# An encoder layer on one core: first-pass weights fetched a pair ahead, weight sums in three steps, a buffer pool moved, output row tiles alternated

## The chip, the core and the metric

The kernel runs on one core of one Trainium2 chip, in float32. The metric is the device time of one execution in microseconds (us). The engines each work through a queue of their own in order: PE (TensorE) multiplies matrices, DVE (VectorE) and ACT (ScalarE) work elementwise, SP (SyncE) issues nearly all DMAs.

## The reference

```python
mod = jax.nn.silu(c) @ w_ada + b_ada
shift, scale, gate = jnp.split(mod, 3, axis=-1)
h = rmsnorm(x, pre_g) * (1.0 + scale[:, None]) + shift[:, None]
q, k, v, gate_a, u, gate_p = jnp.split(h @ w_in, SPLIT_POINTS, axis=-1)
y_a = windowed_gqa(q, k, v, rel_table, sink) * jax.nn.silu(gate_a)
y_p = multiscale_pool(u, w_pool_grp, pool_scale) * jax.nn.silu(gate_p)
g_a, g_p = jnp.split(jax.nn.sigmoid(h @ w_merge + b_merge), 2, axis=-1)
merged = g_a * (y_a @ w_br_attn) + g_p * (y_p @ w_br_pool)
return x + gate[:, None] * rmsnorm(merged @ w_out, post_g)
```

There are 1024 rows of x, the model width is 2048, the combined projection is 4608 columns wide and the merge projection 4096; y_a and y_p are 1024 wide. Everything is float32. The attention sees 128 keys on either side; the pool takes windows of 2 to 16 rows.

## The kernel before, in words

A float32 product is made of three products in a rounded format (float32r). Each operand is split into a high part, written by ACT (L91), and a low part, the rest, written by DVE (L92); PE adds high by high, low by high and high by low. Both parts of a weight are called `whi` and `wlo`, those of the moving operand by the name of the operand and an h or l (`T4h`, `T4l`).

On top of that, a block product of 2 by 2 blocks is made of seven products instead of eight (Strassen's scheme in Winograd's form, `strassen`). The moving operands of the seven are, in order, B11, T3, T2, B21, T4, T1 and B22; their weights are blocks of the weight matrix and sums of blocks (`ws`, or `raw` overwritten). Three PSUM accumulators X, Z and V take the products; ACT and DVE copy and add them up (`p7`, `u2`, `u4`, and results called `c`, `u`, `p`). One such unit, called a pair, makes 256 columns and is 84 matmuls of 128x512 on PE. `load_raws` loads a pair's two raw weight tiles of 512 KB into a ring of 4 buffers.

The program in order of time:

- **Start.** x is normalised and transposed, the modulation is begun, and the first 4 pairs are done in halves.
- **Pass 1** (`pass1`, L590). 34 pairs of columns of w_in and w_merge over the first half of the contraction; partial results go to memory (`part_d`). The first 22 pairs after the start have work between their products: steps of a queue called `side` (columns of w_ada times the conditioning, with a column sum `PM` of 8 small matmuls at the end of each four sets; the gate's rows `gada`, `gacc`), and 16 `weight_sums`. One of those loads four blocks of w_out (`sw`), makes S3, S2, S1 and S4 of them on DVE, and stores them (`ws_d`) for the output product. `pass1` hands one of the 16 to each of the first 16 pairs: loads at its first product, sums and stores at its sixth.
- **Pass 2.** The second half of the contraction over the 34 pairs, with attention and pooling between the products.
- **Branch products.** y_a times w_branch_attn, then y_p times w_branch_pool, 8 pairs each. A result is multiplied by a gate tile `gt` (loaded from memory, then a sigmoid on ACT, L1018); the first branch's results go to memory (`mp_d`), the second's are added to tiles `m` and `pv` loaded from there. Before the second branch the pool of copies `ev3` is closed and two pools are made in its place and that of the closed source pool `ysrc` (the rows `y`): `mraw`, which holds `m`, first and `ev4` behind it. So `ev4` and `ev3` are at different addresses.
- **Output product** (`out_pair`, four of them: two row halves by two column sets). The moving operand and the weight trade places here: the 128 rows of m are loaded into PE (`mh`, `ml`), and the weight tile moves. Each of the seven products has 8 contraction tiles for 2 row tiles, 48 matmuls. Weights are loaded (`wr`, 512 KB holding two contraction tiles, a ring of 4) and split (ring of 4 `whi`, 4 `wlo`). `out_mm` (L1091) takes one `wr` at a time: 6 matmuls for row tile 0, then 6 for row tile 1. Copies live in a pool `ev5`, made when `ev4` closes.
- **The end.** Rows are normalised, scaled and added to x (`row_scale`, `finish_block`, L1116) and stored. In the last `out_pair` the product S4 has its eight weight tiles all split beforehand, into buffers of a large pool (`wzh`, `wzl`), and is done row tile by row tile, so that row tile 6 is finished while 7 is multiplied. The finishing of row tiles 4 and 5 stands behind the fifth product.

A scheduler sets each engine's queue from the order in which the code emits instructions, their priorities and its own model of time; the built program is then fixed.

Of the kernel before, what the change touches and what calls it, by code (L numbers as in the profile page):

```python
# [20 lines left out]
P = 128  # L21
# [21 lines left out]
def encoder_layer(ctx: ExitStack, tc: tile.TileContext, x, c, table, w_ada, b_ada, pre_g,  # L43
# [546 lines left out]
    def pass1(n, side, every, at=()):  # L590
        nonlocal i
        at = iter(at)
        for k in range(n):
            w, n0 = weight_of(ORDER[i])
            run(strassen(w, n0, rows_in_turn(0), range(4), op, ev, to_dram(block(part_d, ORDER[i]))),
                side, every[k % len(every)], next(at, ()))
            i += 1
        flush()
# [8 lines left out]
    def weight_sums(j, i):  # L607


        a = {}  # L610
# [7 lines left out]
        def make():  # L618
# [5 lines left out]
            for name, t in (("S3", a["21"]), ("S2", s2), ("S1", a["11"]), ("S4", a["12"])):  # L624
                store(ws_rows(name)[:, j, i * 512:(i + 1) * 512], t)

        return (0, fetch), (5, make)
# [61 lines left out]
    sums = [weight_sums(j, n) for n in range(2) for j in range(KT // 2)]  # L689
    pass1(-(-2 * len(side) // 7), side, EASY, sums)  # L690
    assert len(sums) <= i - RAMP
# [292 lines left out]
    for b, w in enumerate((w_ba, w_bp)):  # L984
# [4 lines left out]
        else:  # L989
            ysrc.close()  # L990
            ev_ctx.close()
            ev_ctx = ExitStack()
            mr = ctx.enter_context(pool("mraw", side="right"))
            ev = ev_ctx.enter_context(pool("ev4", 4, side="right"))
# [62 lines left out]
    ev_ctx.close()  # L1057
    ev = ctx.enter_context(pool("ev5", side="right"))
    ssq = const.tile([P, NB, 4], F32, name="ssq_o")

    def put_step(n, op, m, t2):

        name = MOVING[n]
        for jp in range(JP):
# [3 lines left out]
            split(hi, lo, src)  # L1068
# [22 lines left out]
    def out_mm(pb, op, name, jp, t, ws, first, last):  # L1091
        ts_ = slice(t * P, (t + 1) * P)
        hi, lo = op[name][jp]
        for x_, n in ((hi, 0), (lo, 0), (hi, 1)):
            for jj in range(2):
                nc.tensor.matmul(pb, x_[:, jj, ts_], ws[jj][n], start=first and x_ is hi and n == 0 and jj == 0,  # L1096
                                 stop=last and n == 1 and jj == 1, skip_group_check=True)
# [29 lines left out]
    def out_pair(half, i, op, after):  # L1127
# [4 lines left out]
        for nh in range(2):  # L1132
            g[nh] = ev.tile([P, 512], F32, tag="pg", name=uid("pg"), bufs=2)
# [3 lines left out]
        def product(wname, mov, pbs, fresh=False, by_rows=False):  # L1137
            made = []
            for jp in range(JP):
                raw = weights(wname, i, jp)  # L1140
                ws = []
                for jj in range(2):
                    if by_rows:
                        hi, lo = slot("wzh"), slot("wzl")
                    else:
                        hi = wp.tile([P, 512], F32R, tag="whi", name=uid("whi"), bufs=4)
# [191 lines left out]
```

## Time and profile before

| | |
|---|---|
| median of 3 runs (2170.9 to 2178.26) | 2170.98 us |
| the profiled execution | 2171.72 us |
| its span in the trace | 2169.9 us |
| mean granted clock of PE | 0.993 |
| PE busy / DVE busy / ACT busy | 97% / 71% / 52% |
| DMA moved | 466.10 MB |

The profiled execution has 1.8 us outside the span of its trace. Times in the text are us from the start of the span. L numbers are lines of the kernel. In a row of the timeline, a number in brackets is the idle time of the engine just before, and the name behind the arrow is what ended it.

### The profile page before, as it was taken

How to read it: one execution, taken by the hardware profiler on the slowest of the kernel's cores; microseconds unless marked ns; L12 is line 12 of the kernel's file. 1: busy time of each engine (PE TensorE's matmuls, PEld its weight loads, DVE VectorE, ACT ScalarE, POOL GpSimd, SP SyncE). 2: the span in 40 equal slices, each digit the busy share in tenths (PEclk: the TensorE clock that was granted, in tenths of full speed). 3: DMA queues.
4: the chain of work that ended last, by engine and by line, in shares of the span. 5: the costliest groups of instructions: out<-in, count | busy, mean ns of one | idle time of the engine just before them, and what ended most of it. 6: DMA issues, size and time to landing. Idle time of an engine off the chain costs nothing. (4 is left out here: it accounts for less than half of the span.)

```text
span 2169.9 us, 28942 instructions
## 1 busy us (share of the span) xinstructions
PE 2108.8 (97%) x9567; PEld 1719.6 (79%) x9567; DVE 1534.2 (71%) x2754; ACT 1123.0 (52%) x2124; POOL 7.5 (0%) x66
## 2 busy tenths in 40 slices
PE   6999999999999999999999999999999899999997
PEld 3588878778888888888888878888788787788776
DVE  5788767766436676777777878557857777878656
ACT  5654434444374546767775433334646444667554
POOL 0000000000000000000000000000000000000000
PEclk9999999999999999999999999999999999999999
DMA  9989989874443356545445766755654654876896
GB/s 329 289 275 331 319 280 321 296 225 148 148 148 110 117 175 200 169 155 183 160 151 185 234 196 210 246 187 176 218 169 147 217 166 153 265 257 212 288 329 209
DMA packets 303254, 466.10 MB, mean 215 GB/s; under 512 B 23882, under 2 KB 144866, under 8 KB 303104
## 3 DMA queue, kind: packets, MB, share of 16 engines
q1 hardware_dynamic: 301648, 462.02, 65.5%
q0 software_dynamic: 1120, 2.19, 0.3%
q8 instruction: 75, 1.23, 0.2%
q14 instruction: 75, 0.61, 0.1%
q10 hardware_dynamic: 336, 0.06, 0.0%
HBM read 340.41 MB, written 125.85 MB: 215 GB/s over the span
## 5 line engine op out<-in xcount | busy, mean ns | idle before, releaser
L91 ACT ACTIVATE whi<-raw 128x512 fp32r<-128x512 f32 (+1 forms) x528 | 320.3, 610 | 507.6 <-PE Z L228 257.7
L92 DVE TENSOR_TENSOR wlo<-raw,whi 128x512 fp32r<-128x512 f32 (+1 forms) x528 | 347.1, 661 | 178.9 <-PE Z L228 119.0
L91 ACT ACTIVATE whi<-wr 128x512 fp32r<-128x512 f32 x216 | 125.5, 624 | 99.2 <-PE V L1096 32.8
L92 DVE TENSOR_TENSOR wlo<-wr,whi 128x512 fp32r<-128x512 f32 x216 | 139.4, 686 | 48.0 <-ACT whi L91 43.5
L95 DVE TENSOR_TENSOR raw<-raw,raw 128x512 f32<-128x512 f32 x80 | 55.2, 690 | 96.0 <-DMA raw<-in_w_merge_dram 62.0
L1018 ACT ACTIVATE gt<-gt,cols 128x512 f32<-128x512 f32 x64 | 45.9, 723 | 108.3 <-DMA gt<-proj_d 91.7
L228 PE MATMUL V<-T4h,whi 128*128 128x512 f32 x336 | 93.2, 396 | 6.5 <-ACT p L238 6.5
L228 PE MATMUL Z<-T1h,whi 128*128 128x512 f32 x336 | 93.0, 395 | 3.6 <-ACT u L238 2.8
L228 PE MATMUL Z<-B22h,whi 128*128 128x512 f32 x336 | 93.6, 398 | 2.7 <-ACT u L283 2.7
L228 PE MATMUL V<-T3h,whi 128*128 128x512 f32 x336 | 92.1, 393 | 2.7 <-DVE u L95 2.6
L228 PE MATMUL X<-B11h,whi 128*128 128x512 f32 x336 | 92.2, 393 | 2.1 <-ACT B11h L91 0.8
L228 PE MATMUL Z<-B22l,whi 128*128 128x512 f32 x336 | 92.5, 395 | 0.0
L228 PE MATMUL V<-T4l,whi 128*128 128x512 f32 x336 | 91.7, 392 | 0.0
L228 PE MATMUL Z<-T1l,whi 128*128 128x512 f32 x336 | 91.6, 392 | 0.0
L228 PE MATMUL V<-T4h,wlo 128*128 128x512 f32 x336 | 91.6, 392 | 0.0
L228 PE MATMUL V<-T3l,whi 128*128 128x512 f32 x336 | 91.6, 392 | 0.0
L228 PE MATMUL X<-B11l,whi 128*128 128x512 f32 x336 | 91.4, 390 | 0.2 <-DVE B11l L92 0.2
L228 PE MATMUL V<-T3h,wlo 128*128 128x512 f32 x336 | 91.4, 392 | 0.0
L228 PE MATMUL Z<-T2h,whi 128*128 128x512 f32 x336 | 91.4, 391 | 0.0
L228 PE MATMUL Z<-T1h,wlo 128*128 128x512 f32 x336 | 91.3, 392 | 0.0
L228 PE MATMUL Z<-B22h,wlo 128*128 128x512 f32 x336 | 91.2, 391 | 0.0
L228 PE MATMUL X<-B21h,whi 128*128 128x512 f32 x336 | 90.9, 390 | 0.0
(314 smaller groups left out, 4751.8 us busy)
## 6 DMA issues: line engine op xcount, KB each, us to landing
part<-part_d SPq DMA_DIRECT2D x136, 256.0 KB, 4.8
ada<-in_w_ada_dram SPq DMA_DIRECT2D x128, 256.0 KB, 5.9
raw<-in_w_in_dram SPq DMA_DIRECT2D x64, 512.0 KB, 4.5
raw<-in_w_merge_dram SPq DMA_DIRECT2D x64, 512.0 KB, 5.2
wr<-ws_dS SPq DMA_DIRECT2D x64, 512.0 KB, 5.3
wr<-in_w_out_dram SPq DMA_DIRECT2D x48, 512.0 KB, 5.6
proj_d<-part SPq DMA_DIRECT2D x68, 256.0 KB, 2.2
sw<-in_w_out_dram SPq DMA_DIRECT2D x64, 256.0 KB, 5.9
```

What stands on the lines that cost most here:

```text
L91: nc.scalar.activation(hi, src, AF.Copy)
L92: nc.vector.tensor_tensor(lo, src, f32(hi), ALU.subtract)
L95: (eng or nc.vector).tensor_tensor(o, a, b, ALU.add)
L228: nc.tensor.matmul(ps, w_[:, i], op[mov][j][m_], start=fresh and i == 0 and n == 0, stop=i == nj - 1 and n == 2, skip_group_check=True)
L1018: nc.scalar.activation(gt, gt, AF.Sigmoid, bias=cols[:, col:col + 1])
```

## The change

Five things are changed.

1. `pass1` fetches the raw weights of the next pair at the third product of each pair, and hands them to `strassen`.
2. A weight sum has three steps (loads, sums, stores) at positions 0, 5 and 7, counted in products, and the 16 sums start at even distances over all 22 pairs instead of one to each of the first 16.
3. `ev4` is made before `mraw`, and is kept to the end: `ev5` is gone. The output product's copies take the buffers of `ev4` (tags gt, ev and pv).
4. `out_mm` takes one contraction tile: 3 matmuls for row tile 0, 3 for row tile 1, and so on; the last two contraction tiles go row tile by row tile. For one of the first operands of the output product, ACT's part of the split is kept in the program's order.
5. In the last `out_pair` the weights of S4 are loaded and split ahead of the copies of S1's result, and the finishing of row tiles 4 and 5 stands behind the sixth product.

```diff
-    def pass1(n, side, every, at=()):
+    ready = []
+
+    def fetch_pair(n):
+        ready.append(load_raws(*weight_of(ORDER[n]), rows_in_turn(0), range(4)))
+
+    def pass1(n, side, every, steps={}):
+
         nonlocal i
-        at = iter(at)
         for k in range(n):
+            if not ready:
+                fetch_pair(i)
+            at = [(at, step) for at, step in ((at, steps.get(7 * k + at)) for at in range(7)) if step]
+            if i + 1 < PAIRS:
+                at.append((2, lambda i=i: fetch_pair(i + 1)))
             w, n0 = weight_of(ORDER[i])
-            run(strassen(w, n0, rows_in_turn(0), range(4), op, ev, to_dram(block(part_d, ORDER[i]))),
-                side, every[k % len(every)], next(at, ()))
+            run(strassen(w, n0, rows_in_turn(0), range(4), op, ev, to_dram(block(part_d, ORDER[i])),
+                         raws=ready.pop(0)), side, every[k % len(every)], at)
             i += 1
         flush()
...
-        a = {}
+        a, done = {}, []
...
             sub(s2, a["22"], a["21"])
             add(a["11"], a["11"], s2)
             sub(a["12"], a["12"], s2)
-            for name, t in (("S3", a["21"]), ("S2", s2), ("S1", a["11"]), ("S4", a["12"])):
+            done.extend((("S3", a["21"]), ("S2", s2), ("S1", a["11"]), ("S4", a["12"])))
+
+        def keep():
+            for name, t in done:
                 store(ws_rows(name)[:, j, i * 512:(i + 1) * 512], t)
-        return (0, fetch), (5, make)
+        return fetch, make, keep
...
-    sums = [weight_sums(j, n) for n in range(2) for j in range(KT // 2)]
-    pass1(-(-2 * len(side) // 7), side, EASY, sums)
-    assert len(sums) <= i - RAMP
+    n1 = -(-2 * len(side) // 7)
+    steps = {}
+    for n, three in enumerate(weight_sums(j, h_) for h_ in range(2) for j in range(KT // 2)):
+        for at, step in zip((0, 5, 7), three):
+            steps[7 * n1 * n // 16 + at] = step
+    assert len(steps) == 48 and max(steps) < 7 * n1
+    pass1(n1, side, EASY, steps)
...
             ev_ctx = ExitStack()
+            ev = ctx.enter_context(pool("ev4", 4, side="right"))
             mr = ctx.enter_context(pool("mraw", side="right"))
-            ev = ev_ctx.enter_context(pool("ev4", 4, side="right"))
...
     merged_sums(mt, mt2, JP - 1)
-    ev_ctx.close()
-    ev = ctx.enter_context(pool("ev5", side="right"))
...
-            split(hi, lo, src)
+            if m is mt and n == 0 and jp == JP - 1:
+                tc.keep_in_program_order(nc.scalar.activation(hi, src, AF.Copy))
+                sub(lo, src, f32(hi))
+            else:
+                split(hi, lo, src)
...
-    def out_mm(pb, op, name, jp, t, ws, first, last):
+    def out_mm(pb, op, name, j, t, w, first, last):
         ts_ = slice(t * P, (t + 1) * P)
-        hi, lo = op[name][jp]
-        for x_, n in ((hi, 0), (lo, 0), (hi, 1)):
-            for jj in range(2):
-                nc.tensor.matmul(pb, x_[:, jj, ts_], ws[jj][n], start=first and x_ is hi and n == 0 and jj == 0,
-                                 stop=last and n == 1 and jj == 1, skip_group_check=True)
+        hi, lo = (o_[:, j % 2, ts_] for o_ in op[name][j // 2])
+        nc.tensor.matmul(pb, hi, w[0], start=first, stop=False, skip_group_check=True)
+        nc.tensor.matmul(pb, lo, w[0], start=False, stop=False, skip_group_check=True)
+        nc.tensor.matmul(pb, hi, w[1], start=False, stop=last, skip_group_check=True)
...
-            g[nh] = ev.tile([P, 512], F32, tag="pg", name=uid("pg"), bufs=2)
+            g[nh] = ev.tile([P, 512], F32, tag="ev", name=uid("pg"))
...
-        def product(wname, mov, pbs, fresh=False, by_rows=False):
-            made = []
+        def split_weights(wname, ring=True):
             for jp in range(JP):
                 raw = weights(wname, i, jp)
-                ws = []
                 for jj in range(2):
-                    if by_rows:
-                        hi, lo = slot("wzh"), slot("wzl")
-                    else:
-                        hi = wp.tile([P, 512], F32R, tag="whi", name=uid("whi"), bufs=4)
-                        lo = wp.tile([P, 512], F32R, tag="wlo", name=uid("wlo"), bufs=4)
+                    hi, lo = (wp.tile([P, 512], F32R, tag=t, name=uid(t), bufs=4) if ring else slot(t)
+                              for t in ("whi", "wlo"))
                     split(hi, lo, raw[:, jj])
-                    ws.append((hi, lo))
-                made.append(ws)
-                if not by_rows:
-                    for t in range(2):
-                        out_mm(pbs[t], op, mov, jp, t, ws, fresh and jp == 0, jp == JP - 1)
-            return made
-
-        def tiles(tag):
-            return [ev.tile([P, 512], F32, tag=tag, name=uid(tag), bufs=2) for _ in range(2)]
+                    yield hi, lo
+
+        def product(wname, mov, pbs, fresh=False):
+
+            ws = split_weights(wname)
+            nj = 2 * JP
+            for j in range(nj - 2):
+                w = next(ws)
+                for t in range(2):
+                    out_mm(pbs[t], op, mov, j, t, w, fresh and j == 0, False)
+            w = list(ws)
+            for t in range(2):
+                for j in (nj - 2, nj - 1):
+                    out_mm(pbs[t], op, mov, j, t, w[j - nj + 2], False, j == nj - 1)
+
+        def tiles(name):
+            tag, bufs = {"p7": ("gt", 4), "u2": ("gt", 4), "c11": ("ev", 4), "u4": ("pv", 2)}[name]
+            return [ev.tile([P, 512], F32, tag=tag, name=uid(name), bufs=bufs) for _ in range(2)]
...
         product("S1", "T1", bz)
+        ws = list(split_weights("S4", ring=False)) if final else None
         u4 = copies([slot("u4", F32) for _ in range(2)] if final else tiles("u4"), bz)
...
-        made = product("S4", "B22", bz, by_rows=True)
         c12 = [slot("c12", F32) for _ in range(2)]
         for t in range(2):
-            for jp in range(JP):
-                out_mm(bz[t], op, "B22", jp, t, made[jp], False, jp == JP - 1)
+            for j, w in enumerate(ws):
+                out_mm(bz[t], op, "B22", j, t, w, False, j == len(ws) - 1)
             result("12", t, bz[t], c12[t])
             scale = row_scale(6 + t)
...
         if n in (2, 4):
-            for T in (n + 2, n + 3) if n == 2 else (6, 7):
+            for T in (4, 5) if n == 2 else (6, 7):
                 for b in range(4):
                     fetch_x_block(T, b, lambda name: slot(name, F32))
-        if n == 4:
+        if n == 5:
             assert not side
             for T in (4, 5):
```

How the built programs differ, at three places. The first is ACT's queue in the second branch product, pair 0, around the sixth product; `p_3198` and `u_3201` are the copies of V and Z, numbers behind names are those of buffers. Before:

```order
L91 ACTIVATE T4h_15598<-y_15132 128x512
L91 ACTIVATE T1h_15602<-y_14443 128x512
L91 ACTIVATE T1h_15606<-y_14649 128x512
L91 ACTIVATE T1h_15610<-y_14882 128x512
L91 ACTIVATE whi_15826<-ws_15824 128x512
L91 ACTIVATE T1h_15614<-y_15087 128x512
L91 ACTIVATE B22h_15618<-y_14560 128x512
L91 ACTIVATE B22h_15622<-y_14765 128x512
L91 ACTIVATE B22h_15626<-y_14971 128x512
L91 ACTIVATE B22h_15630<-y_15204 128x512
L238 ACTIVATE p_3198_15704<-V_15668 128x512
L238 ACTIVATE u_3201_15724<-Z_15667 128x512
```

After:

```order
L91 ACTIVATE whi_15773<-raw_15662 128x512
L238 ACTIVATE p_3198_15704<-V_15668 128x512
L91 ACTIVATE T4h_15590<-y_14721 128x512
L1035 ACTIVATE gt_15650<-gt_15650,cols 128x512
L91 ACTIVATE T4h_15594<-y_14926 128x512
L1035 ACTIVATE gt_15653<-gt_15653,cols 128x512
L91 ACTIVATE T4h_15598<-y_15132 128x512
L1035 ACTIVATE gt_15656<-gt_15656,cols 128x512
L91 ACTIVATE T1h_15602<-y_14443 128x512
L1035 ACTIVATE gt_15659<-gt_15659,cols 128x512
L91 ACTIVATE T1h_15606<-y_14649 128x512
L238 ACTIVATE u_3201_15724<-Z_15667 128x512
```

The copy `p` has moved from behind the split of B22 to ahead of that of T4, and the gates' sigmoids have come in between. DVE's queue at the same place, before:

```order
L92 TENSOR_TENSOR wlo_15827<-ws_15824,whi_15826 128x512
L92 TENSOR_TENSOR T1l_15615<-y_15087,T1h_15614 128x512
L98 TENSOR_TENSOR raw_15800<-raw_15800 128x4x128
L92 TENSOR_TENSOR B22l_15619<-y_14560,B22h_15618 128x512
L98 TENSOR_TENSOR ws_15987<-raw_15963 128x512
L92 TENSOR_TENSOR B22l_15623<-y_14765,B22h_15622 128x512
L92 TENSOR_TENSOR B22l_15627<-y_14971,B22h_15626 128x512
L92 TENSOR_TENSOR B22l_15631<-y_15204,B22h_15630 128x512
L1029 TENSOR_TENSOR c_15742<-X_15666,gt_15650 128x512
L95 TENSOR_TENSOR u_3201_15724<-V_15668,u_3201_15724 128x512
L95 TENSOR_TENSOR m_15642<-m_15642,c_15742 128x512
L1033 TENSOR_TENSOR u_3201_15724<-u_3201_15724,gt_15653 128x512
```

After:

```order
L95 TENSOR_TENSOR u_3201_15724<-V_15668,u_3201_15724 128x512
L92 TENSOR_TENSOR T1l_15615<-y_15087,T1h_15614 128x512
L1050 TENSOR_TENSOR u_3201_15724<-u_3201_15724,gt_15653 128x512
L92 TENSOR_TENSOR B22l_15619<-y_14560,B22h_15618 128x512
L92 TENSOR_TENSOR wlo_15808<-raw_15800,whi_15807 128x512
L92 TENSOR_TENSOR B22l_15623<-y_14765,B22h_15622 128x512
L95 TENSOR_TENSOR p_3198_15704<-p_3198_15704,u_3211_15789 128x512
L92 TENSOR_TENSOR B22l_15627<-y_14971,B22h_15626 128x512
L1050 TENSOR_TENSOR p_3198_15704<-p_3198_15704,gt_15656 128x512
L92 TENSOR_TENSOR B22l_15631<-y_15204,B22h_15630 128x512
L95 TENSOR_TENSOR pv_15793<-pv_15793,p_3198_15704 128x512
L92 TENSOR_TENSOR wlo_15827<-ws_15824,whi_15826 128x512
```

The results `c`, `u`, `p` and `pv` now stand between the low parts of T1 and B22, and `m<-m,c` stands five rows further back.

The second place is SP's queue in pass 1, where the last of the 16 weight sums has its loads (`sw`), at the 17th of the 34 pairs. `gada` are loads for the gate's rows, `raw` those of weights. Before:

```order
L616 DMA sw_4285<-in_w_out_dram 128x512
L616 DMA sw_4287<-in_w_out_dram 128x512
L616 DMA sw_4289<-in_w_out_dram 128x512
L304 DMA part_d<-u_849_3849 128x512
L180 DMA raw_4093<-in_w_merge_dram 128x4x256
L616 DMA sw_4291<-in_w_out_dram 128x512
L304 DMA part_d<-p_842_3807 128x512
L625 DMA ws_dS_97<-sw_4287 128x512
L636 DMA gada_4165<-in_w_ada_dram 128x1024
L636 DMA gada_4208<-in_w_ada_dram 128x1024
L636 DMA gada_4258<-in_w_ada_dram 128x1024
```

After:

```order
L626 DMA sw_5144<-in_w_out_dram 128x512
L638 DMA ws_dS_95<-sw_4894 128x512
L638 DMA ws_dS_98<-sw_4900 128x512
L304 DMA part_d<-u_836_3802 128x512
L180 DMA raw_3941<-in_w_merge_dram 128x4x256
L304 DMA part_d<-p_823_3748 128x512
L626 DMA sw_5146<-in_w_out_dram 128x512
L649 DMA gada_4101<-in_w_ada_dram 128x1024
L649 DMA gada_4149<-in_w_ada_dram 128x1024
L649 DMA gada_4194<-in_w_ada_dram 128x1024
L626 DMA sw_5148<-in_w_out_dram 128x512
L626 DMA sw_5150<-in_w_out_dram 128x512
```

In both programs the last sum's loads stand at about the same row. Before, the four stood ahead of three `gada`; now the last two stand behind them.

The third place is ACT's queue at the end of the program; `u_4218` and `u_4236` are the first copies of S1's result. Before:

```order
L91 ACTIVATE whi_19943<-wr_19941 128x512
L91 ACTIVATE whi_19947<-wr_19941 128x512
L1161 ACTIVATE u_4218_19963<-Z_19325 128x512
L1161 ACTIVATE u_4219_19964<-Z_19326 128x512
L91 ACTIVATE wzh_19977<-wr_19975 128x512
L1105 ACTIVATE junk_19968,ssq_o<-p_4110_19519 128x512
L1105 ACTIVATE junk_19972,ssq_o<-p_4111_19520 128x512
L91 ACTIVATE wzh_19981<-wr_19975 128x512
L91 ACTIVATE wzh_19987<-wr_19985 128x512
```

After:

```order
L1128 ACTIVATE st_19987<-st_19987,eps_t 128x1
L1128 ACTIVATE st_19999<-st_19999,eps_t 128x1
L91 ACTIVATE whi_19951<-wr_19945 128x512
L91 ACTIVATE whi_19957<-wr_19955 128x512
L91 ACTIVATE whi_19961<-wr_19955 128x512
L91 ACTIVATE whi_19967<-wr_19965 128x512
L91 ACTIVATE whi_19971<-wr_19965 128x512
L1183 ACTIVATE u_4236_19975<-Z_19321 128x512
L1183 ACTIVATE u_4237_19976<-Z_19322 128x512
L1123 ACTIVATE junk_19980,ssq_o<-p_4110_19515 128x512
L1123 ACTIVATE junk_19984,ssq_o<-p_4111_19516 128x512
```

The copies `u` stood ahead of the last eight splits, and now stand behind them.

## The prediction

> **What bounds the kernel now.** First the page and the list of what PE waited for.
>
> ```profile
> PE 2108.8 (97%) x9567; PEld 1719.6 (79%) x9567; DVE 1534.2 (71%) x2754; ACT 1123.0 (52%) x2124; POOL 7.5 (0%) x66
> PE V L228 <- ACT p L238: 6.5, 1, 6.5
> PE PM L417 <- DVE acc L463: 4.1, 1, 4.1
> PE X L1096 <- DVE wlo L92: 3.1, 3, 2.2
> PE Z L228 <- ACT u L238: 2.8, 2, 1.9
> PE Z L228 <- ACT u L283: 2.7, 2, 2.5
> PE V L228 <- DVE u L95: 2.6, 1, 2.6
> PE Z L1096 <- ACT wzh L91: 2.5, 2, 1.5
> ```
>
> PE is busy 97% of the span, so only its losses can be won: single waits in few places. What each place costs, with the slow clock after it, is read from the windows (width, busy time and count of each engine, granted clock, DMA share, GB/s) and from PE's pace when it waits for nothing.
>
> ```profile
> 285.00:310.00 25.00, 20.86 (x87) 17.16 (x86) 15.85 (x26) 7.48 (x13) 0.00 (x0) 0.86 0.83 276
> 310.00:425.00 115.00, 115.00 (x512) 95.15 (x511) 84.43 (x125) 47.93 (x78) 0.00 (x0) 1.00 0.91 305
> 425.00:470.00 45.00, 40.44 (x163) 32.43 (x162) 29.99 (x42) 17.06 (x30) 0.00 (x0) 0.92 0.79 256
> ...
> 1680.00:1705.00 25.00, 18.50 (x69) 14.66 (x68) 18.34 (x31) 13.14 (x24) 0.00 (x0) 0.80 0.43 137
> ...
> 1830.00:1850.00 20.00, 15.30 (x59) 11.61 (x59) 17.27 (x29) 8.98 (x17) 0.00 (x0) 0.91 0.47 149
> 1850.00:2090.00 240.00, 236.32 (x1024) 190.91 (x1023) 182.34 (x298) 152.19 (x295) 0.00 (x0) 1.00 0.81 264
> 1682.61 1.07 PE L228 MATMUL X<-B21h,whi 128*128 128x512 f32 x4
> 1683.52 1.07 PE L228 MATMUL X<-B21l,whi 128*128 128x512 f32 x4
> 1684.42 1.07 PE L228 MATMUL X<-B21h,wlo 128*128 128x512 f32 x4
> 1691.99 2.07 PE L228 MATMUL V<-T4h,whi 128*128 128x512 f32 x4 [6.50 <-ACT p L238]
> ```
>
> Eight matmuls take 1684.42 - 1682.61 = 1.81 us, 0.226 each. A window's width less its matmuls at 0.226 is its loss. At 1680 it is 25 - 69 x 0.226 = 9.4 us, at 425 it is 45 - 163 x 0.226 = 8.2, at 1830 it is 20 - 59 x 0.226 = 6.7, and over 1850 to 2090 it is 8.6. At 285, 8 of the 87 are the small PM, for which I allow 0.5 us: 25 - 79 x 0.226 - 0.5 = 6.6. The end follows below.
>
> **The change, part by part.**
>
> *The copies' pool.* ACT, DVE and SP at the second branch product, in that order:
>
> ```profile
> 1688.55 2.17 ACT L91 ACTIVATE B22h<-y 128x512 fp32r<-128x512 f32 x4
> 1691.35 0.60 ACT L238 ACTIVATE p<-V 128x512 f32<-128x512 f32 x1 [0.63 <-DVE B22l L92]
> 1676.19 0.68 DVE L1029 TENSOR_TENSOR c<-Z,gt 128x512 f32<-128x512 f32 x1
> 1690.63 0.68 DVE L92 TENSOR_TENSOR B22l<-y,B22h 128x512 fp32r<-128x512 f32 x1
> 1693.75 1.74 SPq L1016 DMA_DIRECT2D gt<-proj_d  x4
> 1695.53 0.90 SPq L1041 DMA_DIRECT2D m<-mp_d  x2
> 1701.29 0.70 DVE L95 TENSOR_TENSOR m<-m,c 128x512 f32<-128x512 f32 x1 [1.96 <-DMA m<-mp_d]
> ```
>
> PE wanted V's bank for T4 at 1685.3, and `p`, which empties it, came at 1691.35: its buffer lies where the rows `y` were, and it waits for B22l, a reader of them. With `ev4` on the place of `ev3`, `p` needs only buffers whose last readers were done by about 1677 (`c<-Z,gt`, 1676.19), and it stands ahead of T4's splits; so the 9.4 us go. What is late next: DVE now has `c`, `u`, `p`, `pv` between T1l and B22l. DVE runs one operation each 0.60 us (it has no idle time here), and the rows of the order from 1685.2 on put the last T1l at 1690.1 and the last B22l at 1694.9. PE without its wait needs them at 1689.6 and 1692.9: waits of 0.5 and 2.0 us in pieces. The `m` loads still wait for the last reader of `y`, so `m<-m,c` stays at about 1701.3 and holds the weights' low parts behind it to 1703; PE, going on at 1685.3, has 80 matmuls before it needs one (to 1703.4, and the 2.5 on top), so I add 0.5 at most. New losses 3.0, term **-6.4**. Ends: -9.4 if nothing is late, -2 if DVE's stand before `m<-m,c` (1695.5 to 1701.3, 5.8 us) comes out on PE with a slow clock.
>
> *Pass 1.* The two losses of 6.6 and 8.2 us end on DVE. The PE, DVE and SP rows before them:
>
> ```profile
> 292.19 1.07 PE L228 MATMUL Z<-B22h,whi 128*128 128x512 f32 x4
> 297.40 1.84 PE L417 MATMUL PM<-ones,acc 128*128 128x1 f32 x8 [4.14 <-DVE acc L463]
> 416.51 0.69 DVE L98 TENSOR_TENSOR sw<-sw,sw 128x512 f32<-128x512 f32 x1 [3.77 <-DMA sw<-in_w_out_dram]
> 432.83 0.69 DVE L98 TENSOR_TENSOR ws<-raw 128x512 f32<-128x512 f32 x1 [1.82 <-DMA raw<-in_w_merge_dram]
> 426.52 0.52 SPq L180 DMA_DIRECT2D raw<-in_w_merge_dram  x1
> ```
>
> DVE is in order and stands at a load, of a weight sum (3.77 us) or of a weight, which was issued at 426.52 and used at 432.83; what PE wants is queued behind. A weight a pair ahead would take away the second kind. But the built program moves little: the 16 sums still fall in the same 13 pairs, the raw loads were ahead already as far as their 4 buffers let them, and they move past two to five other loads in some five pairs only. The bytes of a pair are the same: 305 GB/s x 19.0 us (84 x 0.226) = 5.8 MB, at a DMA share of 0.91, so queueing stays. Of the PM sums, one of four stalled; the order leaves two of the new positions with a margin below 0.5 us, and the last sum's loads now stand behind three 512 KB loads. Gain end: both losses, -14.8. Loss end: one more stall like the larger, +8. I take **-2**, near nothing, because the order of loads hardly changes, with -10 to +8 as ends for the range, since both stalls going without a new one is the less likely.
>
> *ACT's pinned split* (1830, 6.7 us) changes no engine's order at that place: **0**, with 2 us either way for what reaches it earlier or later. PE's two waits there:
>
> ```profile
> 1838.66 2.08 PE L228 MATMUL Z<-B22h,whi 128*128 128x512 f32 x4 [2.54 <-ACT u L283]
> 1840.54 1.56 PE L228 MATMUL Z<-B22l,whi 128*128 128x512 f32 x4
> 1846.55 0.73 PE L1096 MATMUL X<-wlo,mh 128*128 128x512 f32 x2 [2.16 <-DVE wlo L92]
> ```
>
> *Row tiles alternate.* A product needs the first low part after 2 matmuls instead of 4 (0.45 us earlier), the second after 8 instead of 5 (0.68 later): where DVE is the bound these cancel. Buffers of `whi` and `wlo` come free some 4 matmuls (1 us) earlier, which spreads DVE's work in the third `out_pair`: -1.5. Three times S4 starts on a bank whose copy was taken late, with 3 instead of 6 matmuls between its row tiles: +0.5 each. Sum **0**; the waits of 8.6 us over 1850 to 2090 bound it, I take 3 either way.
>
> *Last weights ahead.* ACT, SP and PE rows of the end, and the DMA view of 2120 to 2150:
>
> ```profile
> 2147.50 1.08 ACT L1161 ACTIVATE u<-Z 128x512 f32<-128x512 f32 x2 [5.66 <-PE Z L1096]
> 2146.94 0.38 SPq L1085 DMA_DIRECT2D wr<-ws_dS  x1
> 2149.16 0.73 PE L1096 MATMUL Z<-wzh,mh 128*128 128x512 f32 x2 [1.46 <-ACT wzh L91]
> 2150.89 0.50 PE L1096 MATMUL Z<-wzh,mh 128*128 128x512 f32 x1 [1.00 <-ACT wzh L91]
> wr<-ws_dS SPq DMA_DIRECT2D x8, 512.0 KB, 4.5
> ```
>
> Before, S4 is split behind the copies and starts in steps; its third matmul at 2150.89 means an unbroken start at 2150.4. After, all of S4 is split when the copies run, but ACT is in order: the last `wr` takes a ring buffer that frees at about 2142.5, lands 4.5 us later (2147.0), two splits of 0.52 follow, then one copy of 0.58: S4 starts at 2148.6. S1 ends at about 2146.5, since eight finishing operations no longer stand ahead of its last low part. So PE waits 2.1 us, once, and the term is 2148.6 - 2150.4 = **-1.8**. Ends: -3.9 with the load in time, +1 with a landing of 6 to 7 us. Whether the clock drops after those 2.1 us decides something too. After the 2.54 us idle at 1838.66 four matmuls took 1.88 us (to 1840.54), 0.47 each; after the 2.16 us at 1846.55 two took 0.73, as after the 1.46 at 2149.16. I take the 2.16, which is nearest, so nothing; by the 2.54, some six matmuls would lose 0.24 each, 1.5 us, and the term would be -0.3.
>
> The Trainium skill (TensorE: Matmul & The Clock Gate, Part 1) says that PE's clock halves after an idle window of about 3.4 us and comes back after as long a busy one. The 2.54 us here did it in less than that, so the trace differs; by that rule the 2.1 us would cost nothing, and the sum stays -10.2.
>
> The new buffers of the output product's copies (gt, ev, pv) have as many or more slots than before, and are on no wait of the list: 0.
>
> Sum: -6.4 - 2 + 0 + 0 - 1.8 = -10.2. Against the profiled execution, 2171.72 - 10.2 = 2161.5; the median is 0.74 lower than that execution, so **2160.8 us**.
>
> **The rivals.**
>
> - *Pass 1 loses its stalls altogether.* For it: both hang on loads that come a few us late. Against: the order of loads hardly moves. -14.8 in place of -2: 2148.
> - *The gap only moves*: gates and `m` come late in place of `p`. For it: `m<-m,c` already waited 1.96 us and holds DVE. Against: the 80 matmuls that PE has in hand. -2 in place of -6.4 for the pool, and no gain in pass 1: 2167.
> - *The first part doesn't do what it says*: the sums aren't spread, the loads are no earlier. 0 in place of -2: 2163.
> - *Slower: pass 1 stalls more often.* The mechanism is DVE standing at a sum's late load while PM or a low part is queued behind. Each stall costs 6.6 to 8.2 us. Two more make 2161 + 2 + 16 = 2179, still within 0.5%; from three more (2187) it is slower. For it: the last sum's loads stand behind three 512 KB loads. Against: two of 16 sums stalled before.
>
> **How the numbers follow.** The forecast has a chance of 0.48, its own range being 2154 to 2167. The others, in the order above: 0.18, 0.14, 0.13, 0.07. Over 0.5% (10.9 us, about what a measurement can tell) faster is below 2160.1: half of the forecast's share (0.24), nearly all of the first rival (0.17), a third of the third (0.04), little of the second (0.01): 0.46. Slower is above 2181.8: 0.05, the last rival less its part with two stalls. The rest, 0.49, is within 0.5%. The range runs from 2145 (the first rival with some 3 us more) to 2175 (one or two more stalls); 0.2 is left out, in the ends.
>
> **What would show it.** In the trace after, the wait of V for `p` of 6.5 us is gone, and waits of at most 2 us for T1l, B22l or `wlo` stand from 1689 to 1705. In pass 1 the row of PM for `acc` (4.1) or that of V for `u` (2.6) is shorter, or there in another pair. The wait at 1838.66 is as long as before. S4 has one wait, for the copy `u`, of about 2 us. The prediction is wrong if pass 1 has no stall over 2 us, or three or more, or if V waits at the second branch product for a gate.

## The result and the profile after

The kernel after takes 2161.92 us (median of 6 runs, 2157.92 to 2163.52), before 2173.89 us on the same chip (2170.7 to 2178.26); the ratio is 0.9942, with a 95% interval of 0.9925 to 0.996, that is 8.7 to 16 us faster. The forecast was 2160.8. The profiled execution took 2163.38 us, 8.3 less than that of before; its span is 2161.6.

The page's line of busy times and the longest of PE's waits of the kernel after (waited for, us in total, times, longest), but for two of 7 to 11 us at the start that both kernels have:

```profile
PE 2101.6 (97%) x9567; PEld 1716.7 (79%) x9567; DVE 1535.7 (71%) x2754; ACT 1129.2 (52%) x2124; POOL 7.5 (0%) x66
PE X L1115 <- DVE wlo L92: 5.7, 2, 3.3
PE PM L417 <- DVE acc L463: 4.9, 2, 2.5
PE Z L1115 <- DVE wlo L92: 4.0, 3, 1.7
PE V L228 <- DVE u L95: 2.9, 3, 1.7
PE Z L1113 <- ACT u L1183: 2.6, 1, 2.6
PE Z L228 <- ACT u L238: 1.8, 1, 1.8
PE V L1115 <- DVE wlo L92: 1.6, 1, 1.6
PE Z L228 <- ACT u L283: 1.2, 2, 0.9
```

The longest wait of before behind the start, 6.5 us of V for `p`, is gone, and the longest that is left there is 3.3 us. The waits of the output product for `wlo` have grown (5.7, 4.0 and 1.6 us; before 3.1, 2.2 and 0.3), and PM waits 4.9 us in two places instead of 4.1 in one. The same windows as before:

```profile
285.00:310.00 25.00, 20.88 (x88) 16.63 (x87) 16.56 (x28) 7.23 (x12) 0.00 (x0) 0.93 0.92 302
310.00:425.00 115.00, 114.65 (x509) 94.60 (x508) 88.17 (x132) 48.04 (x78) 0.00 (x0) 1.00 0.94 309
425.00:470.00 45.00, 45.00 (x199) 36.99 (x198) 33.00 (x46) 20.03 (x35) 0.00 (x0) 1.00 0.85 289
...
1680.00:1705.00 25.00, 24.84 (x110) 20.07 (x109) 23.80 (x41) 18.02 (x33) 0.00 (x0) 1.00 0.60 204
...
1830.00:1850.00 20.00, 16.74 (x74) 13.51 (x73) 18.64 (x32) 13.66 (x25) 0.00 (x0) 1.00 0.63 205
1850.00:2090.00 240.00, 231.86 (x1007) 189.11 (x1006) 177.68 (x287) 151.70 (x284) 0.00 (x0) 0.99 0.81 264
```

From 1680 to 1705 PE starts 110 matmuls instead of 69, at full clock. From 425 to 470 there are 199 instead of 163. From 1850 to 2090 there are 17 fewer.

Windows shift as a kernel gets faster. So the traces are compared by counting: the large matmuls (128x512) are numbered in PE's order, 8626 in each kernel, and the start of the same number is set against that in the profiled run of before. The table gives the change over five stretches, in us, minus meaning faster, one profiled run each. The times in its head are those of before. The rest of a kernel's total, most of it between 487 and 1661 us, lies in code that no kernel changes; only in e7, e10 and e11 do loads of pass 1 reach into it (see e7). In the kernel after the five stretches make -11.3, and this rest +3.0.

```
                    pass 1   2nd branch  to 2077   2077-2111  the end
                   163-487   1661-1709  1709-2077            2111-2161
after                -2.5      -9.1       -3.3       +4.7       -1.1
e1_pool_only         +3.1      -9.2       +0.4        0.0       +2.6
e2_pass1_old         -2.2      -9.1       -1.0       +4.5       +0.1
e3_rows_old          +1.2      -9.0       +0.4       -1.0       +1.5
e4_end_old           -1.0      -9.2       -3.1       +4.7       -0.3
e5_fetch_only         0.0      -9.6       -0.7       +3.1       -1.2
e6_spread_only       +0.2      -9.1       -1.4       +2.5       +3.1
e7_sums_pinned       -8.9      -9.2       -2.1       +1.5       -0.7
e8_x_ahead           -2.1      -9.4       +2.2       -0.3       +0.2
e9_tail              +4.0      -9.6       -3.0       +2.5       -3.8
e10_best            -10.2      -9.6       +2.0       -0.9       -2.4
e11_best_rows_old    -9.8      -9.5       +0.4       -1.0       -3.3
```

One column is needed to read the others: e1 and e2 have pass 1 of before, and still differ from it by +3.1 and -2.2. So a single figure of pass 1 is good to some 3 us, or 4 (e9 has pass 1 of after and stands at +4.0). The second branch repeats within 0.6.

### The profile page after: what moved, and what is told of

It reads as the page before. It is cut to its first block, busy times and chain, and to the rows that moved or that the text cites. A ratio compares the mean times of both kernels' runs of the same rounds, so it can differ in the third digit from the quotient of the medians.

```text
span 2161.6 us, 28949 instructions
## 1 busy us (share of the span) xinstructions
PE 2101.6 (97%) x9567; PEld 1716.7 (79%) x9567; DVE 1535.7 (71%) x2754; ACT 1129.2 (52%) x2124; POOL 7.5 (0%) x66
## 4 chain that ended last, share of the span: by engine, by line
PE 75%; DMA 10%; DVE 9%; issue 2%; ACT 2%; SPq 1%; DVEq 0%; ACTq 0%; POOLq 0%
PE Z L228 25%; PE V L228 16%; PE X L228 16%; DVE wlo L92 2%; PE Z L1115 1%; PE Z L1113 1%; PE Z L1114 1%; DMA mo<-in_x_dram 1%; DMA sw<-in_w_out_dram 1%; PE X L1115 1%; PE V L1115 1%; PE V L1113 1%; PE V L1114 1%; PE X L1113 1%; PE X L1114 1%
## 5 line engine op out<-in xcount | busy, mean ns | idle before, releaser
L91 ACT ACTIVATE whi<-wr 128x512 fp32r<-128x512 f32 x224 | 138.7, 628 | 92.9 <-DVE wlo L92 30.4
L92 DVE TENSOR_TENSOR wlo<-wr,whi 128x512 fp32r<-128x512 f32 x224 | 149.4, 688 | 43.2 <-ACT whi L91 41.0
```

Of the source, the lines that this page charges most:

```text
L91: nc.scalar.activation(hi, src, AF.Copy)
L92: nc.vector.tensor_tensor(lo, src, f32(hi), ALU.subtract)
```

## The experiments

**e1: the pool's place alone**, on the kernel before (with the copies of the output product in ev4, and no ev5).

```diff
-            mr = ctx.enter_context(pool("mraw", side="right"))
-            ev = ev_ctx.enter_context(pool("ev4", 4, side="right"))
+            ev = ctx.enter_context(pool("ev4", 4, side="right"))
+            mr = ctx.enter_context(pool("mraw", side="right"))
```

> The kernel before with the third part alone: ev4 ahead of mraw, ev5 gone, the output product's copies in ev4. Theory (the pool's place made the 6.5 us wait, and nothing late takes its place): the 168 large matmuls around 1680 come 9.1 us earlier, as between the two traces, no wait over 1 us from 1680 to 1705, pass 1 as before with its stalls at 293, 431 and 449; in all -9 to -10 us, ratio 0.9955. Rival 1 (the gap's going depends on the other parts, or a gate or m comes late instead): -2 to -5 us, ratio 0.998 to 0.999. Rival 2 (the later copies' places cost or gain something in the output product): the delta over 1850 to 2090 differs from 0 by more than 1 us.

Measured 2166.74 us against 2173.18, ratio 0.9965 (0.9949 to 0.998). At the second branch -9.2 us, in the output product +0.4: the theory holds there, and both rivals fall. This one edit gives 4.3 to 11 us by the runs; its ratio is 0.35% under 1, that of the whole change 0.58%, so it has the larger part of the gain.

**e2: pass 1 of before**, the rest as after.

```diff
-                         raws=ready.pop(0)), side, every[k % len(every)], at)
+                side, every[k % len(every)], next(at, ()))
...
-        return fetch, make, keep
+        return (0, fetch), (5, make)
```

> The kernel after with pass 1 of before (weights fetched where they are used, sums one to a pair). Theory (pass 1's gain is a balance of stalls lost and won): the stalls at 431 and 449 are back (+7.6 us), those at 194 and 275 are gone (-5.4 us); in all +2.5 us against the kernel after, ratio to before 0.9954. Rival 1 (the stalls at 194 and 275 are chance of the DMA's timing and the part is worth all 7.6): +7 us or more, ratio to before 0.9975. Rival 2 (the part does nothing, all stalls are chance): within 1 us of the kernel after.

2165.4 us, ratio 0.9962 (0.9945 to 0.9979) against 0.9942 (0.9925 to 0.996) of the kernel after. The intervals overlap, so the runs leave open what the part is worth. The traces show the stalls as the theory has them: those at 194 and 275 are gone, and V waits 1.9 us at 432 and Z 1.1 us at 449. But these are shorter in this run than in before, and the sum is -2.2 where 0 was expected: chance of one run moves it as much as the edit.

**e5 and e6: one half of the change in pass 1 each.** e5 has the weights fetched ahead and the sums of before, e6 the sums spread and the weights of before.

```diff
 e5
-        for at, step in zip((0, 5, 7), three):
-            steps[7 * n1 * n // 16 + at] = step
+        for at, step in two:
+            steps[7 * n + at] = step
 e6
-            if i + 1 < PAIRS:
-                at.append((2, lambda i=i: fetch_pair(i + 1)))
```

> The kernel after with the weight sums as before (one to each of the first 16 pairs, two steps), the weights fetched a pair ahead. Theory (both effects of pass 1 come from the fetch: the scheduler puts the next pair's weight sum ws on DVE ahead of the last adds to acc, and the raw loads are in time at 431 and 449): the stalls at 194 and 275 as after (+5.4 us), those at 431 and 449 gone (-7.6 us); PE's large matmul 1848 is 1 to 3 us earlier than before. Rival (the spreading does it): stalls as before, none at 194, those at 431 and 449 there; matmul 1848 as before or later.

> The kernel after with the weights fetched where they are used, the sums spread in three steps. Theory (the fetch does it): no stall at 194, those at 431 and 449 there as before; matmul 1848 within 2 us of before. Rival (the spreading does it): the stall at 194 there, those at 431 and 449 gone, matmul 1848 some 2 us earlier than before.

Windows 180 to 205 and 400 to 470 of before, after, e5 and e6, in this order:

```profile
180.00:205.00 25.00, 25.00 (x116) 20.81 (x115) 20.80 (x36) 10.48 (x17) 0.00 (x0) 1.00 0.99 335
400.00:470.00 70.00, 65.44 (x273) 52.96 (x272) 47.00 (x65) 27.54 (x47) 0.00 (x0) 0.95 0.82 265
180.00:205.00 25.00, 22.47 (x97) 18.27 (x96) 18.22 (x31) 8.20 (x14) 0.00 (x0) 0.93 0.86 282
400.00:470.00 70.00, 69.65 (x307) 57.06 (x306) 52.10 (x73) 30.50 (x52) 0.00 (x0) 1.00 0.88 295
180.00:205.00 25.00, 25.00 (x116) 20.80 (x115) 20.15 (x35) 10.47 (x17) 0.00 (x0) 1.00 0.97 322
400.00:470.00 70.00, 64.66 (x271) 52.29 (x270) 48.12 (x67) 27.88 (x47) 0.00 (x0) 0.95 0.83 267
180.00:205.00 25.00, 21.76 (x87) 17.78 (x86) 16.45 (x28) 7.41 (x12) 0.00 (x0) 0.86 0.86 283
400.00:470.00 70.00, 70.00 (x310) 57.97 (x309) 52.12 (x74) 31.38 (x53) 0.00 (x0) 1.00 0.87 294
```

My theory falls and the rival holds: e5, with the fetch, looks like before (116 matmuls and no stall at 194, stalls at 431 and 447), and e6, with the spreading, like after (a stall at 194, none from 400 to 470). The ratios are 0.995 (0.9934 to 0.9966) and 0.9954 (0.9939 to 0.9969). The spreading moved the stalls from one end of pass 1 to the other, and the net of it is not distinguishable from nothing: over pass 1 the five kernels with both halves (after, e3, e4, e8, e9) have a mean of -0.1 us, those with neither (e1, e2, and before as 0) +0.3.

**e7: the sums spread for good.** Each load of a sum is held on SP's queue behind everything that the program has issued there before it, so that the scheduler can't draw it forward.

```diff
-                load(a[name], wo_rows(kh)[:, j, n0:n0 + 512])
+                tc.keep_in_program_order(load(a[name], wo_rows(kh)[:, j, n0:n0 + 512]))
```

> The kernel after with each load of a weight sum pinned on SP's queue behind what the program has issued before it: the sums now lie over all 22 pairs, the last one's loads some 60 rows of SP's queue later. Theory (the stalls come from loads that queue behind each other in the 13 dense pairs and DVE standing at them): the GB/s from 150 to 420 falls from about 300 to about 270, the waits for PM and for u fall by more than half, 4 to 8 us faster than the kernel after. Rival 1 (the stalls come from the order on DVE, not from the density): the stalls at 194 and 300 stay, within 2 us. Rival 2 (sums that reach further put new stalls where pairs 17 to 26 are quiet now): stalls after 450, 2 us or more slower.

2160.31 us against 2175.71, ratio 0.9931 (0.991 to 0.9951). Windows of e7, and last the one from 470 of the kernel after:

```profile
205.00:285.00 80.00, 80.00 (x359) 66.35 (x358) 58.95 (x94) 33.25 (x54) 0.00 (x0) 1.00 0.83 273
285.00:310.00 25.00, 24.75 (x113) 20.33 (x112) 16.18 (x27) 9.87 (x16) 0.00 (x0) 1.00 0.74 233
310.00:400.00 90.00, 90.00 (x402) 74.53 (x401) 66.95 (x100) 37.33 (x61) 0.00 (x0) 1.00 0.85 280
470.00:560.00 90.00, 89.77 (x404) 73.04 (x402) 56.83 (x81) 37.42 (x62) 2.28 (x3) 1.00 0.75 244
470.00:560.00 90.00, 90.00 (x399) 73.40 (x398) 50.07 (x68) 37.41 (x62) 2.28 (x3) 1.00 0.54 168
```

The sums now reach past 470 (244 GB/s instead of 168), the stretch before runs at 233 to 280 GB/s instead of about 300, and PE stalls no more at 276, 297 and 302; the stall at 194 stays (2.3 us), and those at 431 and 449 were gone in the kernel after already. Over pass 1 this is -8.9 us, and -10.2 and -9.8 in e10 and e11, which have the same edit: well outside what pass 1 does by chance, and 6 to 8 us better than the kernel after. But part of it is paid back behind pass 1, as the second rival has it in kind. From 520 to 700 us every other kernel is within 0.1 us of before, and these three lose 1.3, 1.6 and 4.6. DVE stands at the load of a sum there, and PE behind it; DVE's and PE's rows of e11:

```profile
523.50 0.69 DVE L98 TENSOR_TENSOR sw<-sw,sw 128x512 f32<-128x512 f32 x1 [3.01 <-DMA sw<-in_w_out_dram]
526.63 1.20 PE L228 MATMUL V<-T3h,whi 128*128 128x512 f32 x4 [1.90 <-DVE u L95]
```

So where the sums' loads stand on SP's queue decides where pass 1 stalls, and spreading them ends the stalls near 300. That the density of the loads made those is not shown: the edit also changes which load stands behind which, the kernel before ran from 180 to 205 at 335 GB/s without a stall, and the new ones came at 215 to 224 GB/s (from 520 to 560). By the runs alone e7's interval still overlaps that of after.

**e3: the row tiles as before**, the rest as after.

```diff
-            for j in range(nj - 2):
-                w = next(ws)
-                for t in range(2):
-                    out_mm(pbs[t], op, mov, j, t, w, fresh and j == 0, False)
+            for jp in range(JP):
+                w = [next(ws), next(ws)]
+                for t in range(2):
+                    two_mm(pbs[t], op, mov, jp, t, w, fresh and jp == 0, jp == JP - 1)
```

> The kernel after with the row tiles of the output product as before: two contraction tiles at a time, 6 matmuls for a row tile. Theory (the second low part is wanted after 8 matmuls instead of 5, but the first after 2 instead of 4, and where DVE is late PE stands longer at the first): the waits of X, V and Z for wlo from 1908 to 2100 fall, the 4.5 us lost there come back, and the kernel is 3 to 5 us faster than the kernel after; ratio to before 0.992. Rival 1 (those waits come from the finishing steps and their loads, whatever the order of matmuls): within 1 us of the kernel after, waits for wlo as long at the same places. Rival 2 (the alternation gained and something else lost): slower than the kernel after by 2 us or more.

Ratio 0.9947 (0.9928 to 0.9966), the same as after within the interval. In the trace the 4.7 us lost from 2077 to 2111 are gone (-1.0), but so are the 3.3 us won before (+0.4). Both together are +1.4 in the kernel after (mean of after, e2, e4 to e7 and e9: +1.3, from -0.6 to +3.5) and -0.3 without the alternation (e3 and e11 -0.6, e1 +0.4). By these means the alternation gives earlier and takes later, and costs 1 to 2 us; this is not 3 to 5. The time is that of the first rival, but its waits are not there as long: those for `wlo` from 2030 on are 1.1 us at most. What PE stands at is seen in SP's, DVE's and PE's rows of the kernel after:

```profile
2070.46 0.46 SPq L1139 DMA_DIRECT2D mo<-in_x_dram  x1
2077.92 0.75 DVE L1134 SCALAR_TENSOR_TENSOR mo<-mo,st 128x512 f32<-128x512 f32 x1 [4.69 <-DMA mo<-in_x_dram]
2079.33 0.56 PE L1115 MATMUL X<-wlo,mh 128*128 128x512 f32 x1 [2.45 <-DVE wlo L92]
2079.69 0.63 PE L1113 MATMUL X<-whi,mh 128*128 128x512 f32 x1
2080.11 0.63 PE L1114 MATMUL X<-whi,ml 128*128 128x512 f32 x1
```

A finishing step of the rows stands on DVE and waits 4.69 us for x, whose load was issued 7.5 us before; the low part of the next weight is behind it. PE waits 2.45 us for that, and its next matmuls start 0.43 us apart instead of 0.226, nine of them, which costs 1.7 us more. In e3 DVE stands at x too (4.45 us at 2062.50, 2.17 at 2078.17), and PE waits 1.1 us or less. So the loss takes both, the late x and the alternation.

**e8: x two steps ahead.**

```diff
-            side.append(lambda: (todo[0][0](), todo[1][0]()))
-            for a_, b_ in zip(todo, todo[2:]):
+            side.append(lambda: (todo[0][0](), todo[1][0](), todo[2][0]()))
+            for a_, b_ in zip(todo, todo[3:]):
                 side.append(lambda a_=a_, b_=b_: (b_[0](), a_[1]()))
+            side.append(todo[-3][1])
```

> The kernel after with the rows of x and o for the finishing steps of the third out_pair fetched two steps ahead instead of one. Theory (the loss of 4.5 us from 2077 to 2111, and the waits for wlo from 2040 on, come from DVE standing at the load of x, 4.7 us at 2078, and the alternation only brought that step forward): the waits of PE for wlo from 2030 to 2100 fall from 7 us to under 2, and the kernel is 5 to 8 us faster than the kernel after. Rival (the alternation itself makes PE want wlo too early): waits at 2040, 2056, 2066 and 2077 of 1 us or more remain, under 2 us gained.

2158.78 us against 2175.71, ratio 0.9926 (0.9907 to 0.9945); the interval overlaps that of after. In the trace the loss from 2077 to 2111 is gone (-0.3), but the stretch before has lost 5.5 us against after (+2.2). Of these, 3.5 lie between 1709 and 2025, for the most part in 13 matmuls 0.43 us apart behind a wait for `wlo` at 1830, where no x is loaded. From 2025 to 2111, where the edit works, e8 is 3.0 us faster than after, and e10, which has the edit too, 3.4. A line of PE's waits and two of DVE's rows of e8:

```profile
PE V L1115 <- DVE wlo L92: 2.9, 1, 2.9
2035.40 0.75 DVE L1134 SCALAR_TENSOR_TENSOR mo<-mo,st 128x512 f32<-128x512 f32 x1 [2.91 <-DMA mo<-in_x_dram]
2038.65 0.75 DVE L1134 SCALAR_TENSOR_TENSOR p<-p,st,mo 128x512 f32<-128x512 f32 x1 [2.50 <-DMA mo<-in_x_dram]
```

DVE still stands at x here, as in the kernel after (1.19 us at 2035.82, 3.09 at 2040.26), and PE waits 2.85 us behind it; from 2052 to 2111 it stands at x no more, but 3.25 us at a load of o at 2066.98, where PE waits 0.4 us. So a step more of lead ended the loss from 2077 on and left the waits ahead of it: 3 of the 5 to 8 us came. Why the earlier loads still come late was not tried.

**e4: the end as before** (S4's weights split behind the copies, row tiles 4 and 5 finished behind the fifth product).

```diff
-        ws = list(split_weights("S4", ring=False)) if final else None
         u4 = copies([slot("u4", F32) for _ in range(2)] if final else tiles("u4"), bz)
...
+        ws = list(split_weights("S4", ring=False))
         c12 = [slot("c12", F32) for _ in range(2)]
```

> The kernel after with the end as before: S4 split behind the copies of S1's result, row tiles 4 and 5 finished behind the fifth product. Theory (the traces' difference at the end): +1.1 us against the kernel after, with waits of 1.6 and 1.2 us for wzh and 0.6 for wlo instead of one of 2.8 for the copy u. Rival (the later finishing of tiles 4 and 5, or their stores, cost or gain elsewhere, from 2090 on): a difference of over 2 us in either direction from 2090 to the end.

Ratio 0.995 (0.9929 to 0.9971); the end is at -0.3 us, 0.7 worse than after. The theory's 1.1 is within what the kernels with the new end scatter (after, e2, e3, e5 to e8: -1.2 to +3.1, mean +0.3; old end, before, e1 and e4: 0, +2.6, -0.3). Most of that scatter is PE's clock behind the wait at the start of S4. Windows behind that wait in the kernel after and in e6 (the number before the last two is the granted clock):

```profile
2142.00:2145.00 3.00, 3.00 (x14) 2.44 (x15) 3.00 (x6) 1.58 (x5) 0.00 (x0) 1.00 0.47 175
2142.00:2145.00 3.00, 2.28 (x5) 1.82 (x6) 3.00 (x7) 1.64 (x4) 0.00 (x0) 0.50 0.58 217
```

e1 and e6 have a half clock for 6.8 us there, e2, e3 and e8 for 3.4, and the others none. Without it the new end is at -1.1, -1.2 and -0.7 (after, e5, e7) and the old at 0 and -0.3 (before, e4). So this part is worth some 0.8 us at full clock, and 0.5 by the means of all, which the scatter does not tell from nothing.

**e9: six of S4's eight weight tiles ahead of the copies, two behind.**

```diff
-        ws = list(split_weights("S4", ring=False)) if final else None
+        if final:
+            made = split_weights("S4", ring=False)
+            ws = [next(made) for _ in range(2 * JP - 2)]
...
             result("22", t, p7[t], p7[t])
+        if final:
+            ws.extend(made)
```

> The kernel after, but in the last out_pair only six of S4's eight weight tiles are split ahead of the copies u of S1's result, the last two behind them. Theory (ACT is in order, and the copies wait behind the splits of the last load): the wait of Z for u falls from 2.8 us to about 0.8 (one copy), nothing is late behind it, and the end comes 1.5 to 2.5 us earlier than in the kernel after, from 2099 on. Rival (S4 then stands at its seventh weight tile, which still comes late): a wait for whi or wlo of 1 us or more inside S4, gain under 1 us.

The rows of ACT and PE in the kernel after, then those of ACT in e9:

```profile
2140.19 1.15 ACT L91 ACTIVATE whi<-wr 128x512 fp32r<-128x512 f32 x2 [1.69 <-DMA wr<-ws_dS]
2141.24 1.07 ACT L1183 ACTIVATE u<-Z 128x512 f32<-128x512 f32 x2
2141.88 0.50 PE L1113 MATMUL Z<-whi,mh 128*128 128x512 f32 x1 [2.64 <-ACT u L1183]
```

```profile
2140.50 1.16 ACT L91 ACTIVATE whi<-wr 128x512 fp32r<-128x512 f32 x2 [0.94 <-DMA wr<-ws_dS]
2141.56 1.32 ACT L1183 ACTIVATE u<-Z 128x512 f32<-128x512 f32 x2
2143.22 0.63 ACT L91 ACTIVATE whi<-wr 128x512 fp32r<-128x512 f32 x1 [0.34 <-DMA wr<-ws_dS]
```

In the kernel after the copies stand behind two splits that wait for the last load until 2140.19, and PE, out of work since about 2139, waits 2.64 us. In e9 that load is used behind the copies, and S4 starts with no wait of 0.5 us or more. The end is at -3.8, and at -2.4 and -3.3 in e10 and e11, where waits of 0.9 and 0.5 us for `u` are left: 1.3 to 2.7 us better than after, near the theory's 1.5 to 2.5. The time of e9 does not show it (0.9945, 0.9924 to 0.9965; this profiled run lost 4.0 us in pass 1).

**e10 and e11: the edits of e7, e8 and e9 together**, e11 also with the row tiles as before.

> The kernel after with three further edits: sums' loads pinned, rows of x two steps ahead, six of S4's weight tiles ahead of the copies. Theory (the three losses lie in different places and add up): 7.7 + 4.4 + 2 = 14 us faster than the kernel after, ratio to before 0.988. Rival (runs differ by as much, and stalls reappear elsewhere): ratio 0.991 or more, one of the places keeps its loss.

> The same three edits, with the row tiles as before (two contraction tiles at a time). Theory (with the rows of x in time the alternation neither costs nor gains more than 1 to 2 us): within 2 us of the alternating version. Rival 1 (the alternation costs by itself): 3 us or more faster. Rival 2 (it gains by itself): 3 us or more slower.

e10: 2153.44 us against 2175.89, ratio 0.9906 (0.9888 to 0.9924). e11: 2152.41 us, ratio 0.9896 (0.9878 to 0.9913), the fastest here. Both intervals lie apart from that of the kernel after, e10's by a hair. The page of e11:

```profile
span 2151.6 us, 28928 instructions
PE 2102.4 (98%) x9567; PEld 1716.4 (80%) x9567; DVE 1534.7 (71%) x2754; ACT 1122.7 (52%) x2124; POOL 7.4 (0%) x66
```

Against the kernel after e10 gains about 8 us and e11 about 10 by the ratios, where 14 were expected. In the traces of e10 and of after pass 1 gives 7.7 us and loses 1.6 right behind it, x gives 3.4 of its 4.4, and the end 1.3 of 2. That is 11; the trace of e10 also lost 4.2 us more than that of after between 700 and 1661, in code that is the same, and 3.2 from 1709 to 2025. The two versions agree within their intervals, so the alternation's 1 to 2 us are not settled by the runs.

## Why the prediction was right, and where it was wrong

The total was right (-10.2 forecast for the profiled run, -8.3 measured there, and -12 between the medians), but partly by terms that offset each other.

- **The pool: -6.4 forecast, -9.1 measured**, in all twelve kernels that have it -9.0 to -9.6. The mechanism is the one described. The size was off since I let PE need B22l at 1692.9, right behind T1, and took 2.0 us for that. PE's queue has the next pair's B11 and T3 in between, and had them in the kernel before too (there T1 is done by 1700.48, where B11 starts, and B22 starts at 1705.92). Rows of ACT, PE and DVE of the kernel after:

```profile
1680.36 0.60 ACT L238 ACTIVATE p<-V 128x512 f32<-128x512 f32 x1 [0.21 <-PE V L228]
1685.60 1.07 PE L228 MATMUL V<-T4h,whi 128*128 128x512 f32 x4
1690.29 0.50 PE L228 MATMUL Z<-T1l,whi 128*128 128x512 f32 x1 [0.16 <-DVE T1l L92]
1691.56 1.07 PE L228 MATMUL X<-B11h,whi 128*128 128x512 f32 x4
1697.94 1.09 PE L228 MATMUL Z<-B22l,whi 128*128 128x512 f32 x4
1699.12 0.69 DVE L95 TENSOR_TENSOR m<-m,c 128x512 f32<-128x512 f32 x1 [1.00 <-DMA m<-mp_d]
```

  So B22l was needed at 1697.9 and ready at 1695.1. Of the three new waits only that for T1l is there, with 0.16 us, and `m` held DVE for 1.0 us with PE unharmed. The end "nothing is late" (-9.4) was the case.
- **Pass 1: -2 forecast, -2.5 in the trace, about 0 over the kernels.** The size stands, the reason does not. I held that the built order hardly changes and that the fetch would do what was done. The spreading did it, by a new stall of PM at 194 and by the end of those at 431 and 449. The range's thought that PM margins below 0.5 us could fail was right. The step that failed is the one that weighs an order by how far its rows moved: few rows moved, and 13 us of stalls changed place. Rival three (the part does not do what it says) was right in this: the fetch alone (e5) changes nothing that can be told from chance, and the sums reach past 470 only with their loads pinned (e7). The luck is in the size: -2 was taken as near nothing, and -2.5 is the sum of +5.4 and -8.2 in one run of several.
- **The pinned split: 0 forecast.** e3 and e11 have it without the alternation, e1 has neither, and all three stand at +0.4 to 2077: no effect of it is seen. But the sign that I named there failed. The wait at 1838.66 was to be as long as before (2.54 us), and is 0.89 in the kernel after, while the one behind it has grown from 2.16 to 3.26:

```profile
1827.70 1.20 PE L228 MATMUL Z<-B22h,whi 128*128 128x512 f32 x4 [0.89 <-ACT u L283]
1835.34 0.73 PE L1115 MATMUL X<-wlo,mh 128*128 128x512 f32 x2 [3.26 <-DVE wlo L92]
```

  With 0.58 us just ahead of them they make 4.73 us, as against 4.70 before, so the loss stayed and changed its place. It goes with the alternation: without it (e1, e3, e11) the first wait is 1.9 to 2.2 us, with it 0.9.
- **Row tiles: 0, with 3 either way; measured +1.4 over the stage.** The sum held; the two parts, -3.3 and +4.7, were larger than I wrote (-1.5 and +1.5), and the second had another cause: DVE at a load of x, not S4's bank, and 1.7 us of it is the half clock behind that.
- **The end: -1.8 forecast, -1.1 measured**, -0.5 to -0.8 by the other kernels. The mechanism is shown by e9, with a wait of 2.64 us where 2.1 was forecast. No half clock followed it in the kernel after, as I took from the nearest row, but that was luck: of the seven kernels with a wait of 2 us or more for `u` at this place four had one (e2, e3, e6 and e8).

## What to carry to other kernels

Where a scheduler builds the queues, spreading loads in the code does not spread them on the chip: read the built queue, and hold the loads where they are meant to be. An engine that works in order passes each late load on to everything behind it, so put what waits for a load behind what the matmuls want next (here copies ahead of the last splits, which e9 shows; finishing steps behind the next low parts would be the same, and were not tried). A copy of a buffer that shares addresses with a live operand waits for that operand's last reader; a pool's place alone was worth 9 us here.

## What the runs showed of the hardware

One program's time differs from run to run more than expected: before took 2165.3 to 2180.5 us over 29 runs beside e1 to e4. In the traces the same pass 1 gained or lost 3 to 4 us, and code that is unchanged, 700 to 1661 us, moved by -3.3 (e8) to +6.3 us (e10). An edit worth 2 or 3 us is seen in a trace at its own place, but not in the time.

Part of that is PE's clock. At half clock matmuls start 0.43 us apart instead of 0.226, and by the traces' record of the granted clock every such stretch, but for the last one of a program, lasts 3.41, 6.83 or 10.24 us. The length of a wait alone does not say whether one follows. At the start of S4 one followed waits of 2.20, 2.26 and 2.31 us (e3, e2, e8), and none followed waits of 2.55, 2.64 and 3.02 us (e5, after, e7).
